# Moving the sample group of a GLA mixer from the front of its stage to between its last two groups, and loading two constants earlier

## The chip, the cores and the metric

The kernel runs on one core of a Trainium2 chip. The metric is the device time of one launch in microseconds (us), lower is better. Three runs of the kernel before took 3023.51, 3023.68 and 3024.13 us; the median is 3023.68.

The engines are named as in the profile: PE is TensorE's matrix multiplication, PEld its weight load, DVE VectorE, ACT ScalarE, POOL GpSimd, and SP SyncE, which in this kernel issues most of the DMAs. Each engine works through its own instructions in order and waits on semaphores for the others.

## What is computed

One layer of a hybrid decoder trunk, for a prompt of 2048 tokens and a sample group of 8 sequences of 8 tokens (64 tokens). Three mixers read the same projected stream: a gated DeltaNet (A), an RG-LRU (B) and a gated linear attention, GLA (C). Their outputs, side by side, go through one output projection with a layer norm, and then through a gated feed-forward block with a causal convolution (ConvFFN). The part that the change touches is mixer C and the output projection. Cut from the reference (chunks of 64 tokens; a chunk of the sample group is one sequence of 8):

```python
def step(S, inp):                       # GLA, one chunk
    qi, ki, vi, fi = inp
    b = jnp.cumsum(fi, axis=-2)
    ...
    att = jnp.einsum('bhik,bhjk,bhijk->bhij', qi, ki, dec)
    o = jnp.einsum('bhik,bhkv->bhiv', qi * jnp.exp(b), S) + jnp.einsum('bhij,bhjv->bhiv', att, vi)
    S_new = jnp.exp(b_last[..., 0, :])[..., None] * S + jnp.einsum('bhjk,bhjv->bhkv', ki * jnp.exp(b_last - b), vi)
    return S_new, o
...
heads = jnp.concatenate([oa, ob, oc], axis=-1)
x = layer_norm(ALPHA * x + heads @ w_out, ln1_g, ln1_b)
f, fconv_new = conv_ffn(x, st_fconv, ffn_w_up, ffn_conv_w, ffn_conv_b, ffn_w_down)
x = layer_norm(ALPHA * x + f, ln2_g, ln2_b)
```

The prompt starts from a state of zero and carries it from chunk to chunk. Each of the 8 sample sequences has a state of its own, given as input (`s_gla`) and returned (`o_glas`).

## The kernel before

`program` runs five stages: `setup`, `phase1` (the input projections), `window_a` (DeltaNet and RG-LRU), `window_c` (mixer C, output projection and first layer norm) and `phase3` (ConvFFN). The stages follow each other in the program, but a scheduler lays out each engine's instructions by priority and dependences, so work of neighbouring stages mixes. Only `phase3` is under `manual_schedule`, where the written order counts within the stage. What a tile waits for is decided by the pools: a tile that is placed where an earlier tile of a closed pool lay waits for all readers of that one.

**Mixer C (`Gla`).** The tokens are cut into groups: `G[0]` to `G[7]` with 256 prompt tokens each, and `G[8]` with the 64 sample tokens. `load` fetches a group's gates, keys, queries (`b`, `k`, `q`) and values (`v`). `prep` builds, head by head (six heads), the scaled copies of keys and queries at three levels (tiles `K1`, `Q1` and so on, filled by ACT and POOL in two sets of slots), takes the scores on PE (tile `s`, L1373), and copies them into `RC`; it transposes values (`pv`, L1394, into `XC`) and keys (`pk`, L1399, into `KC`) with the identity `c_ident`. `RC`, `XC` and `KC` are rings of two for the prompt's groups; the sample has its own `RCs`, `XCs`, `KCs`. `chain` runs the prompt's four chunks of a group in sequence: state product `cs` (L1427), outputs `po` (L1430), norm (L1205 to L1210, with a product by `ones`, L1206).

**The sample (`sample`)** is a generator with two parts. The first loads the eight states into a `room` of four tiles, takes the outputs (L1451 and L1453) and their norm. The second makes the new states: masked values, 8 x 6 matmuls `ss` (L1466) into one bank of PSUM with the tag `cs`, an addition on DVE, and the stores to `o_glas`. In before the room is four spare tiles of `Project` (`spare`: `mx`, `mh`, `ml`, `xt`).

**The output projection (`Project`).** `weights` loads the 8 blocks of `w_out` (`wos`, 512 KB each, three buffers shared with `x`) and splits each in two: `woh` on ACT (L1495), `wol` on POOL and DVE (L1496). A call P(t0) handles 128 tokens: ACT's cast `mh` and POOL's rest `ml` of the mixed heads `mx`, 48 matmuls `pm` (L320) in two halves, then DVE's residual and layer norm. P(2048) is the sample's call, P(0) to P(1920) the prompt's. `transposed` turns the result with the identity (`pt`, L1549), copies it out through the only buffer `xt` (L1550, ACT), and stores it to `s_x1T` (L1552, SP) for phase 3. The calls run at a much lower priority than the mixer, so the scheduler fills PE's gaps with them.

**The order in `window_c`** is `G[8]`, `G[0]`, ..., `G[7]`: the sample is prepared and put out first, the weights are loaded behind it, and its state sums come in G0's turn. The constants `ident` and `ones` for this stage are loaded into a pool `c3` that is opened after `Project`'s pools.

**The start of phase 3.** Its first pool `fx0` takes space that the closed pools of the earlier stages leave. `load_x(0)` loads eight input blocks `fxl00` to `fxl07` from `s_x1T` (the first five issued by POOL, the others by SP, L1666), ACT casts each into `fxh` (L1667), and DVE or, for the blocks 1, 4 and 7, POOL leaves the rest in `fxl` (L1668). The first weights `wh_g`, `wl_g`, `wh_v`, `wl_v` are split by ACT (L1614) and POOL (L1615). With them begin the matmuls `pug` and `puv` (L320).

Of the kernel before, what the change touches and what calls it, by code (L numbers as in the profile page):

```python
# [8 lines left out]
F32 = mybir.dt.float32  # L9
# [294 lines left out]
def load_consts(E, pool, names):  # L304
    t = {}
    for n in names:
        o, w = _CST[n]
        t[n] = pool.tile([128, w], F32, name="c_" + n)
        E.nc.sync.dma_start(t[n], E.d["consts"][:, o:o + w])
    return t  # L310
# [397 lines left out]
def deltanet(E, ctx, pools, need, ahead):  # L708
# [341 lines left out]
    for gs in pairs:  # L1050
        for g in gs:
            prep(g)
        inverse(gs)
        ahead(gs[0].pair)
        for g in gs:
            blocks(g)
        last = gs[-1].smp
        for g in (gs[0], *gs[2:], gs[1]):
            tokens(g)
            weights(g)  # L1060
            if g.b == 7:
                with tc.high_priority(-100):
                    sample()
            if not g.smp:
                chain(g)
# [147 lines left out]
class Gla:  # L1213
# [4 lines left out]
    def __init__(self, E, ctx):  # L1218
        nc, tc = E.nc, E.tc
        self.E = E  # L1220
        E.aset(LNEXP)
        early = ctx.enter_context(tc.tile_pool(name="ce", bufs=1))
        self.early = ctx.enter_context(tc.tile_pool(name="cf", bufs=2))
        pool = ctx.enter_context(tc.tile_pool(name="c1", bufs=1))
        self.tr = ctx.enter_context(tc.tile_pool(name="c2", bufs=2))
        self.pg = {t: ctx.enter_context(tc.tile_pool(name="c" + t, bufs=1, space=PSUM)) for t in ("s", "tk", "g")}
        self.C = load_consts(E, early, ["m2", "m3", "m2s", "bj", "i32"])

        def ring(name, n, c, w):
            return [pool.tile([128, 6, c, w], F32, name=f"{name}{i}") for i in range(n)]  # L1230

        self.RC, self.XC, self.KC = ring("RC", 2, 4, 64), ring("XC", 2, 4, 64), ring("KC", 2, 4, 32)
        sg = [early.tile([128, 6, 1, 64], F32, name="RCs")], ring("XCs", 1, 1, 64), ring("KCs", 1, 1, 32)
        self.slots = [{n: early.tile([128, 256], F32, name=f"{n}_{i}") for n in ("K1", "Q1", "K2", "Q2", "K3", "Q3")}
                      for i in range(2)]
        self.sls = [{n: early.tile([128, 64], F32, name=f"{n}_s{i}") for n in ("K2", "Q2")} for i in range(2)]

        self.KN = [{l: early.tile([128, 512 >> t], F32, name=f"KN{l}_{t}") for l in (1, 2, 3)} for t in range(2)]

        self.DD = [{l: early.tile([128, n, 6], F32, name=f"D{l}_{i}") for l, n in ((1, 4), (2, 16), (3, 64))}  # L1240
                   for i in range(2)]
        self.ebs = pool.tile([32, 6, 8], F32, name="ebs")
        for r in sg:
            nc.vector.memset(r[0][0:64], 0.0)
        nc.vector.memset(sg[0][0][64:], 0.0)
        for d in self.sls + self.KN + self.slots:
            for w in d.values():
                nc.gpsimd.memset(w, 0.0)
        for d in self.DD:
            for w in d.values():  # L1250
                nc.gpsimd.memset(w, 1.0)
        for w in self.RC + self.XC + self.KC:
            nc.gpsimd.memset(w[0:64], 0.0)
        self.G = []
        for g in range(9):
            o = Env()
            o.g, o.smp, o.t0 = g, g == 8, g * 256
            o.RC, o.XC, o.KC = (r[0] for r in sg) if o.smp else (r[g % 2] for r in (self.RC, self.XC, self.KC))
            o.nch = 1 if o.smp else 4
            o.n = 64 * o.nch  # L1260
            self.G.append(o)
# [158 lines left out]
    def chain(self, g):  # L1420
        nc = self.E.nc
        for c in range(4):
            if c % 2 == 0:
                po, z = self.outputs(g.t0 + 64 * c)
            ps = self.psum(f"cs{g.g}{c}", (32, 6, 64), "cs", 1)
            for h in range(6):
                nc.tensor.matmul(ps[:, h], g.KC[:, h, c], g.XC[:, h, c], start=True, stop=True)  # L1427
            for h in range(6):
                p, h2 = divmod(h, 2)
                nc.tensor.matmul(po[h2 * 64:(h2 + 1) * 64, p, c % 2 * 64:c % 2 * 64 + 64], g.XC[:, h, c],  # L1430
                                 g.RC[:, h, c], start=True, stop=True)
            if c < 3:
                nx = g.XC[0:32, :, c + 1]
            else:
                nx = self.G[g.g + 1 if g.g < 7 else 0].XC[0:32, :, 0]
            nc.scalar.copy(nx, ps)
            if g.g == 7 and c == 3:
                nc.sync.dma_start(self.E.d["o_glap"], nx)
            if c % 2 == 1:
                self.norm(po, z, g.t0 + 64 * (c - 1))  # L1440

    def sample(self, g, room):
        nc, E, C = self.E.nc, self.E, self.C
        S0 = big = room
        for i in range(4):
            nc.sync.dma_start(S0[i][0:32], E.d["s_gla"][:, 2 * i:2 * i + 2])
        po, z = self.outputs(g.t0)
        for h in range(6):
            p, h2 = divmod(h, 2)
            o = po[h2 * 64:(h2 + 1) * 64, p]  # L1450
            nc.tensor.matmul(o, g.XC[64:, h, 0], g.RC[64:, h, 0], start=True, stop=False)  # L1451
            for b in range(8):
                nc.tensor.matmul(o[:, b * 8:(b + 1) * 8], S0[b // 2][0:32, b % 2, h],  # L1453
                                 g.RC[0:32, h, 0, b * 8:(b + 1) * 8], start=False, stop=b == 7)
        self.norm(po, z, g.t0)
        yield
        for i in range(4):
            nc.vector.tensor_tensor(big[i][64:], g.XC[64:, None, :, 0].to_broadcast([64, 2, 6, 64]),
                                    C["bj"][64:, 2 * i:2 * i + 2, None, None].to_broadcast([64, 2, 6, 64]), op=OP.mult)
            nc.vector.tensor_tensor(S0[i][0:32], S0[i][0:32],  # L1460
                                    self.ebs[:, :, 2 * i:2 * i + 2, None].rearrange("p h b o -> p b h o")
                                    .to_broadcast([32, 2, 6, 64]), op=OP.mult)
            for b in range(2):
                ps = self.psum(f"ss{i}{b}", (32, 6, 64), "cs", 1)
                for h in range(6):
                    nc.tensor.matmul(ps[:, h], g.KC[64:, h, 0], big[i][64:, b, h], start=True, stop=True)  # L1466
                nc.vector.tensor_tensor(S0[i][0:32, b], S0[i][0:32, b], ps, op=OP.add)
            nc.sync.dma_start(E.d["o_glas"][:, 2 * i:2 * i + 2], S0[i][0:32])
        yield
# [6 lines left out]
class Project:  # L1476
# [13 lines left out]
    def weights(self):  # L1490
        E, nc = self.E, self.E.nc
        for k in range(KD):
# [2 lines left out]
            nc.scalar.copy(self.wh[:, k], st)  # L1495
            (nc.gpsimd if k % 2 else nc.vector).tensor_tensor(  # L1496
                self.wl[:, k], st, self.wh[:, k].bitcast(F32), op=OP.subtract)

    def spare(self):

        tags = [("mx", 2), ("mh", 2), ("ml", 2), ("xt", 1)]
        return [self.tr.tile([128, 2, 6, 64], F32, tag=t, bufs=b, name="sp" + t) for t, b in tags]

    def dest(self, t0):

# [49 lines left out]
def window_c(E):  # L1555

    with ExitStack() as ctx:
        C = Gla(E, ctx)
        P = Project(E, ctx)
        C.C.update(load_consts(E, ctx.enter_context(E.tc.tile_pool(name="c3", bufs=1)), ["ident", "ones"]))  # L1560
        room = P.spare()
        C.dest = P.dest
        order = [C.G[8]] + C.G[:8]
        C.load(order[0])
        for i, g in enumerate(order):
            if i < 8:
                C.load(order[i + 1])
            C.prep(g)
            if g.smp:
                smp = C.sample(g, room)  # L1570
                next(smp)
                P.weights()
            else:
                if g.g == 0:
                    next(smp)
                C.chain(g)
            for t0 in range(g.t0, g.t0 + g.n, 128):
                with E.tc.high_priority(-10 ** 5):
                    P(t0)
                    P.transposed(C.C["ident"], 1)  # L1580
        P.transposed(C.C["ident"])
# [373 lines left out]
def program(tc, dram):  # L1955

    E = Env()
    E.nc, E.tc, E.d = tc.nc, tc, dram
    with ExitStack() as ctx:
        setup(E, ctx)  # L1960
        phase1(E)
        window_a(E)
        window_c(E)
        phase3(E)
# [16 lines left out]
```

## Time and profile before

| what | number |
|---|---|
| median of three runs | 3023.68 us |
| profiled run, its own time | 3025.96 us |
| span of its profile, first to last instruction | 3024.2 us |
| mean granted clock of TensorE | 0.958 |
| PE busy | 2886.8 us (95%) |
| DVE, ACT, POOL busy | 1510.9 (50%), 1231.4 (41%), 844.2 us (28%) |
| first matmuls of P(2048) | 1083.41 us |
| first matmul of P(0) | 1133.94 us |
| first transposes behind the last projection matmul | 1493.23 us |

A row of the timeline gives the start, the duration, engine, line, operation, result and operands, shape and count of merged instructions, and in brackets how long the engine was idle before and what ended that. A name loses its number in the profile, so `pm` stands for all calls of P, and `c_ident` for the identity in each stage. The granted clock (PEclk) is the share of TensorE's full speed that the profile shows as granted. A window from 1040 to 1494 us covers mixer C and the projection; phase 3 takes the rest of the span, half of it all.

### The profile page before, as it was taken

Reading aid. Unit: us, or ns where it says so; the run is one execution under the profiler, and the core shown is the slowest. Engines: PE = TensorE matmul, PEld = TensorE weight load, DVE = VectorE, ACT = ScalarE, POOL = GpSimd, SP = SyncE. Lnnn points to the kernel's source line nnn. Section 1 sums busy time; section 2 is a strip of 40 time slices with the busy share of each in tenths; the row PEclk is TensorE's granted clock in tenths of the full one; section 3 lists DMA queues with packets and bytes.
Section 4 is the critical chain, followed back from the end, with each engine's and each line's share of the span. In section 5 each row is a group of like instructions: output and inputs, shape, how many; then the busy total and the mean of one; then the engine's idle time right before and its main releaser. Section 6 shows DMA issues by size and latency. Waiting matters only on the chain.

```text
span 3024.2 us, 45238 instructions
## 1 busy us (share of the span) xinstructions
PE 2886.8 (95%) x17755; PEld 2490.4 (82%) x17755; DVE 1510.9 (50%) x2454; ACT 1231.4 (41%) x2591; POOL 844.2 (28%) x898
## 2 busy tenths in 40 slices
PE   8999999788889799999899999999999999999998
PEld 7888789777779577767678888888889999999997
DVE  4564443577663676756533333333376443344436
ACT  4474443446653687766332222222232222222223
POOL 0000001734423545444222222222232222222224
PEclk9999999789999579999899999999999999999999
DMA  6221113533433443533531111111134111111111
GB/s 198 83 74 68 58 59 96 144 101 111 114 95 99 108 130 110 150 112 117 180 116 45 46 56 49 51 48 42 49 112 146 42 52 47 48 42 42 49 43 62
DMA packets 196508, 256.77 MB, mean 85 GB/s; under 512 B 43170, under 2 KB 162040, under 8 KB 196232
## 3 DMA queue, kind: packets, MB, share of 16 engines
q1 hardware_dynamic: 194168, 246.58, 26.6%
q0 software_dynamic: 1984, 7.12, 0.6%
q8 instruction: 140, 2.29, 0.3%
q14 instruction: 72, 0.59, 0.1%
q10 hardware_dynamic: 144, 0.20, 0.0%
HBM read 183.94 MB, written 60.08 MB: 81 GB/s over the span
## 4 chain that ended last, share of the span: by engine, by line
PE 60%; DVE 4%; ACT 2%; DMA 1%; issue 1%; POOL 1%; SPq 0%; DVEq 0%; POOLq 0%; ACTq 0%
PE pug L320 16%; PE pd L320 15%; PE puv L320 15%; PE pm L320 6%; PE s L1373 2%; DVE y L1788 1%; PE pd L1870 1%; PE cs L1427 1%; ACT Q L1360 1%; PE zp L1121 1%; PE po L1206 0%; PE zp L1122 0%; PE po L1430 0%; PE zp L1123 0%; DVE act L1724 0%
## 5 line engine op out<-in xcount | busy, mean ns | idle before, releaser
L1724 DVE SCALAR_TENSOR_TENSOR act<-G,cols,act 128x1024 f32<-128x1024 f32 (+1 forms) x132 | 123.6, 950 | 492.0 <-ACT act L1722 489.6
L1877 DVE TENSOR_TENSOR y<-y,pd 128x512 f32<-128x512 f32 x322 | 220.9, 687 | 203.2 <-PE pd L320 196.7
L1615 POOL TENSOR_TENSOR wl_d<-ws_d,wh_d 128x1024 fp32r<-128x1024 f32 x44 | 106.2, 2414 | 569.9 <-ACT wh_d L1614 523.1
L320 PE MATMUL pd<-wh_d,hh 128*128 128x512 f32 x704 | 215.4, 391 | 5.6 <-DVE y L1877 3.7
L320 PE MATMUL pd<-wh_d,hl 128*128 128x512 f32 x704 | 214.9, 390 | 0.0
L320 PE MATMUL pd<-wl_d,hh 128*128 128x512 f32 x704 | 214.6, 390 | 0.0
L1704 ACT COPY G<-pug 128x512 f32<-128x512 f32 (+2 forms) x110 | 55.0, 501 | 388.2 <-PE pug L320 388.2
L320 PE MATMUL pug<-fxh,wh_g 128*128 128x512 f32 (+2 forms) x880 | 198.0, 354 | 3.3 <-ACT wh_g L1614 2.6
L320 PE MATMUL puv<-fxh,wh_v 128*128 128x512 f32 (+2 forms) x880 | 196.4, 352 | 0.8 <-ACT wh_v L1614 0.8
L320 PE MATMUL puv<-fxh,wl_v 128*128 128x512 f32 (+2 forms) x880 | 196.2, 352 | 0.2 <-POOL wl_v L1615 0.2
L320 PE MATMUL puv<-fxl,wh_v 128*128 128x512 f32 (+2 forms) x880 | 196.0, 351 | 0.0
L320 PE MATMUL pug<-fxl,wh_g 128*128 128x512 f32 (+2 forms) x880 | 196.0, 351 | 0.0
L320 PE MATMUL pug<-fxh,wl_g 128*128 128x512 f32 (+2 forms) x880 | 195.9, 351 | 0.0
L320 PE MATMUL pm<-xh,wh 128*128 128x448 f32 (+1 forms) x800 | 181.9, 360 | 7.1 <-ACT xh L370 6.3
L1614 ACT CAST wh_d<-ws_d 128x1024 fp32r<-128x1024 f32 x44 | 45.8, 1040 | 337.5 <-PE pd L1870 173.3
L320 PE MATMUL pm<-xh,wl 128*128 128x448 f32 (+1 forms) x800 | 181.6, 359 | 0.0
L320 PE MATMUL pm<-xl,wh 128*128 128x448 f32 (+1 forms) x800 | 179.8, 358 | 0.5 <-DVE xl L371 0.4
L1766 DVE TENSOR_TENSOR hl<-act,hh 128x512 fp32r<-128x512 f32 (+2 forms) x110 | 124.0, 1128 | 99.5 <-ACT hh L1758 99.5
L320 PEld LDWEIGHTS pug<-fxh,wh_g 128*128 128x128 f32 x880 | 157.0, 189 | 19.0 <-ACT wh_g L1614 3.0
L320 PEld LDWEIGHTS puv<-fxh,wh_v 128*128 128x128 f32 x880 | 156.0, 188 | 14.9 <-ACT wh_v L1614 1.2
L320 PEld LDWEIGHTS pm<-xh,wh 128*128 128x128 f32 x800 | 144.4, 188 | 28.5 <-issue 10.1
L320 PEld LDWEIGHTS puv<-fxh,wl_v 128*128 128x128 f32 x880 | 155.6, 188 | 14.3 <-POOL wl_v L1615 0.6
(731 smaller groups left out, 6273.9 us busy)
## 6 DMA issues: line engine op xcount, KB each, us to landing
ws_d<-in_w_dn SPq DMA_DIRECT2D x44, 512.0 KB
ws_g<-in_w_up SPq DMA_DIRECT2D x43, 512.0 KB
ws_v<-in_w_up SPq DMA_DIRECT2D x43, 512.0 KB
zx<-in_xT SPq DMA_DIRECT2D x56, 256.0 KB
ws<-in_w_in SPq DMA_DIRECT2D x19, 512.0 KB
K<-KN SPq DMA_DIRECT2D x288, 32.0 KB
x<-in_x SPq DMA_DIRECT2D x16, 512.0 KB
s_x<-x SPq DMA_DIRECT2D x16, 512.0 KB
```

The source lines that it names most:

```text
L320: nc.tensor.matmul(ps, w[k], x[k], start=first and i == 0, stop=last and i == 3 * n - 1)
L1121: nc.tensor.matmul(ps, wh[:, k], xl, start=k == 0, stop=False)
L1360: nc.scalar.copy(v4(Q3[32 * a:32 * a + 32], 1)[:, :, a], v4(qq, 1)[:, :, a])
L1373: nc.tensor.matmul(ps[64:, c], K[:, i], Q[:, i], start=True, stop=True)
L1427: nc.tensor.matmul(ps[:, h], g.KC[:, h, c], g.XC[:, h, c], start=True, stop=True)
L1614: nc.scalar.copy(h, t)
L1615: nc.gpsimd.tensor_tensor(lo, t, h.bitcast(F32), op=OP.subtract)
L1704: nc.scalar.copy(G[:, 2 + o:2 + o + m], p[:, :m])
L1724: nc.vector.scalar_tensor_tensor(dst(act), src(i), taps[i], dst(act), op0=OP.mult, op1=OP.add)
L1766: nc.vector.tensor_tensor(dst, act[:, c], hh[:, c].bitcast(F32), op=OP.subtract)
L1788: nc.vector.scalar_tensor_tensor(y[:m, js], y[:m, js], mv[:m, tt, i:i + 1], a[:m, js], op0=op, op1=OP.add if i else OP.mult)
L1877: nc.vector.tensor_tensor(y, y, ps, op=OP.add)
```

## The change

In `window_c` the groups now run in the order `G[0]` to `G[6]`, `G[8]`, `G[7]`. The sample's first part comes in the turn of `G[8]`, its state sums after the chain of `G[7]`. The weights of the projection are loaded behind the preparation of the first group, which is now `G[0]`. The room for the sample's states is no longer spare tiles of `Project` but the halves of `RC[0]` and `XC[0]`, which are G6's. The state sums use the PSUM bank with the tag `tk`, that of the value and key transposes, instead of `cs`. The last state of the chain, which went to the buffer of `G[0]`, now goes to that of `G[7]` itself. The constants `ident` and `ones` are loaded with mixer C's other constants into its first pool `ce`.

```diff
--- before.py
+++ after.py
@@ -1224,7 +1224,7 @@
         pool = ctx.enter_context(tc.tile_pool(name="c1", bufs=1))
         self.tr = ctx.enter_context(tc.tile_pool(name="c2", bufs=2))
         self.pg = {t: ctx.enter_context(tc.tile_pool(name="c" + t, bufs=1, space=PSUM)) for t in ("s", "tk", "g")}
-        self.C = load_consts(E, early, ["m2", "m3", "m2s", "bj", "i32"])
+        self.C = load_consts(E, early, ["m2", "m3", "m2s", "bj", "i32", "ident", "ones"])
 
         def ring(name, n, c, w):
             return [pool.tile([128, 6, c, w], F32, name=f"{name}{i}") for i in range(n)]
@@ -1432,7 +1432,7 @@
             if c < 3:
                 nx = g.XC[0:32, :, c + 1]
             else:
-                nx = self.G[g.g + 1 if g.g < 7 else 0].XC[0:32, :, 0]
+                nx = self.G[min(g.g + 1, 7)].XC[0:32, :, 0]
             nc.scalar.copy(nx, ps)
             if g.g == 7 and c == 3:
                 nc.sync.dma_start(self.E.d["o_glap"], nx)
@@ -1461,7 +1461,7 @@
                                     self.ebs[:, :, 2 * i:2 * i + 2, None].rearrange("p h b o -> p b h o")
                                     .to_broadcast([32, 2, 6, 64]), op=OP.mult)
             for b in range(2):
-                ps = self.psum(f"ss{i}{b}", (32, 6, 64), "cs", 1)
+                ps = self.psum(f"ss{i}{b}", (32, 6, 64), "tk", 1)
                 for h in range(6):
                     nc.tensor.matmul(ps[:, h], g.KC[64:, h, 0], big[i][64:, b, h], start=True, stop=True)
                 nc.vector.tensor_tensor(S0[i][0:32, b], S0[i][0:32, b], ps, op=OP.add)
@@ -1495,11 +1495,6 @@
             nc.scalar.copy(self.wh[:, k], st)
             (nc.gpsimd if k % 2 else nc.vector).tensor_tensor(
                 self.wl[:, k], st, self.wh[:, k].bitcast(F32), op=OP.subtract)
-
-    def spare(self):
-
-        tags = [("mx", 2), ("mh", 2), ("ml", 2), ("xt", 1)]
-        return [self.tr.tile([128, 2, 6, 64], F32, tag=t, bufs=b, name="sp" + t) for t, b in tags]
 
     def dest(self, t0):
 
@@ -1557,23 +1552,25 @@
     with ExitStack() as ctx:
         C = Gla(E, ctx)
         P = Project(E, ctx)
-        C.C.update(load_consts(E, ctx.enter_context(E.tc.tile_pool(name="c3", bufs=1)), ["ident", "ones"]))
-        room = P.spare()
         C.dest = P.dest
-        order = [C.G[8]] + C.G[:8]
+
+        order = [*C.G[:7], C.G[8], C.G[7]]
+        room = [t.rearrange("p h c i -> p (h c i)")[:, i * 768:(i + 1) * 768].rearrange("p (b h i) -> p b h i", b=2, h=6)
+                for t in (C.RC[0], C.XC[0]) for i in range(2)]
         C.load(order[0])
         for i, g in enumerate(order):
-            if i < 8:
+            if i + 1 < len(order):
                 C.load(order[i + 1])
             C.prep(g)
+            if i == 0:
+                P.weights()
             if g.smp:
                 smp = C.sample(g, room)
                 next(smp)
-                P.weights()
             else:
-                if g.g == 0:
-                    next(smp)
                 C.chain(g)
+            if g.g == 7:
+                next(smp)
             for t0 in range(g.t0, g.t0 + g.n, 128):
                 with E.tc.high_priority(-10 ** 5):
                     P(t0)
```

How this moves the instructions is seen in the order of each engine. (The lines behind the change have numbers that are 3 to 5 lower.) First PE around the start of P(0), whose first matmuls are `pm00` and `pm01`; `s1_2` is the score of head 2 of group 1, `po256` the output of tokens 256 to 383. In before:

```order
L1373 MATMUL s2_0_11620<-Q1_0_9705,K1_0_9704 64x64 x4
L1430 MATMUL po256_11219<-RC1_9696,XC1_9698 64x64 x7
L1373 MATMUL s32_0_11621<-Q3_0_9709,K3_0_9708 64x64 x4
L1427 MATMUL cs13_11282<-XC1_9698,KC1_9700 32x64 x6
L1399 MATMUL pk21_11593<-c_ident_9792,kd1_2_11529 64x64 x4
L320 MATMUL pm00_10707<-woh_9780,mh0_10703 128x512 x8
```

and in the changed kernel:

```order
L1373 MATMUL s1_1_10620<-Q2_1_9717,K2_1_9716 64x64 x4
L1373 MATMUL s1_2_10658<-Q1_0_9709,K1_0_9708 64x64 x4
L1373 MATMUL s31_2_10659<-Q3_0_9713,K3_0_9712 64x64 x4
L1430 MATMUL po256_10789<-RC1_9700,XC1_9702 64x64
L1399 MATMUL pk21_11163<-c_ident_9695,kd1_2_11099 64x64 x4
L1427 MATMUL cs20_11400<-XC0_9701,KC0_9703 32x64 x4
L320 MATMUL pm00_10291<-woh_9784,mh0_10287 128x512 x6
```

P(0) stood behind scores of G2's head 0; now it stands behind those of G1's head 2. The sample's matmuls, which stood ahead of both in before, are not ahead of it now. They stand among G7's heads, with the state sums (`ss`) and P(2048) (`pm2048`) between the scores of `s7` and the outputs of the last 256 tokens (`po1792`, `po1920`):

```order
L320 MATMUL pm20481_14378<-woh_9784,ml2048_14349 128x512 x2
L1373 MATMUL s37_4_14716<-Q3_0_9713,K3_0_9712 64x64 x4
L1430 MATMUL po1792_14770<-RC1_9700,XC1_9702 64x64
L1430 MATMUL po1920_14816<-RC1_9700,XC1_9702 64x64
L1466 MATMUL ss30_14922<-XC0_9701,KCs0_9707 32x64 x6
L320 MATMUL pm20481_14378<-woh_9784,ml2048_14349 128x512 x2
L1373 MATMUL s7_4_14715<-Q2_0_9711,K2_0_9710 64x64 x4
L320 MATMUL pm20481_14378<-woh_9784,ml2048_14349 128x512 x4
L320 MATMUL pm20481_14378<-wol_9785,mh2048_14348 128x512 x8
```

Next PE where the projection ends and phase 3 begins (`pm19201` is the last half of P(1920), `pug` the first product of phase 3). In before:

```order
L320 MATMUL pm19201_15056<-wol_9781,mh1920_15026 128x512 x8
L1549 MATMUL pt17920_15093<-c_ident_9792,x1792_14886 128x128 x4
L1549 MATMUL pt17921_15099<-c_ident_9792,x1792_14886 128x128 x4
L320 MATMUL pug0_0_0_15226<-fxl00_15171,wh_g0_0_15164 128x512
L320 MATMUL pug0_0_0_15226<-fxh01_15175,wh_g0_0_15164 128x512
L320 MATMUL pug0_0_0_15226<-fxh01_15175,wl_g0_0_15165 128x512
```

and in the changed kernel:

```order
L320 MATMUL pm19201_15049<-wol_9785,mh1920_15019 128x512 x8
L1544 MATMUL pt17920_15086<-c_ident_9695,x1792_14803 128x128 x4
L1544 MATMUL pt17921_15092<-c_ident_9695,x1792_14803 128x128 x4
L1544 MATMUL pt19200_15100<-c_ident_9695,x1920_14850 128x128 x4
L1544 MATMUL pt19201_15106<-c_ident_9695,x1920_14850 128x128 x4
L320 MATMUL pug0_0_0_15218<-fxh00_15162,wh_g0_0_15156 128x512
L320 MATMUL pug0_0_0_15218<-fxh00_15162,wl_g0_0_15157 128x512
L320 MATMUL pug0_0_0_15218<-fxl00_15163,wh_g0_0_15156 128x512
```

In before two `pug` already stand further up, and 28 more come ahead of the last transposes `pt1920`. Now all four last transposes come first, and every `pug` is behind them. Last ACT at the same place; in before the casts `fxh` are spread among the copies, the last copies `xt1920` stand behind them all:

```order
L1550 COPY xt1792_15092<-pt17920_15093 128x512
L1550 COPY xt1792_15092<-pt17921_15099 128x512
L1667 CAST fxh05_15195<-fxl05_15196 128x1024
L1667 CAST fxh06_15200<-fxl06_15201 128x1024
L1667 CAST fxh07_15205<-fxl07_15206 128x1024
L1614 CAST wh_v0_0_15210<-ws_v0_0_15157 128x1024
L1179 ACTIVATE mv1920_15082<-mv1920_15082 128x1
L1180 ACTIVATE mv1920_15082<-mv1920_15082 128x1
L1550 COPY xt1920_15106<-pt19200_15107 128x512
L1550 COPY xt1920_15106<-pt19201_15113 128x512
```

and in the changed kernel:

```order
L1545 COPY xt1792_15085<-pt17920_15086 128x512
L1545 COPY xt1792_15085<-pt17921_15092 128x512
L1179 ACTIVATE mv1920_15075<-mv1920_15075 128x1
L1180 ACTIVATE mv1920_15075<-mv1920_15075 128x1
L1545 COPY xt1920_15099<-pt19200_15100 128x512
L1545 COPY xt1920_15099<-pt19201_15106 128x512
L1664 CAST fxh00_15162<-fxl00_15163 128x1024
L1664 CAST fxh01_15167<-fxl01_15168 128x1024
L1664 CAST fxh02_15172<-fxl02_15173 128x1024
```

All eight casts now stand behind the copies `xt1920`, each of which needs the buffer that the store of `xt1792` releases. On POOL the rows at this place are the same in both, with the loads `fxl00` and `fxl01` behind `ml1920`; but the first of them, which in before waited for early DMAs of mixer C alone, now also waits for PE's `pt19201`, the last reader of the identity.

## The prediction

> **What bounds the kernel now.** I read first the windows by stage (columns: busy us and instructions of each engine, then the granted clock, DMA share, GB/s), because the change touches only the stage of mixer C, from 1040 to 1494 us, and the hand-over to phase 3 behind it.
>
> ```profile
> core 0: us, PE busy (x) PEld busy (x) DVE busy (x) ACT busy (x) POOL busy (x), PEclk, DMA share, GB/s
> 1040.00:1090.00 50.00, 43.68 (x300) 35.34 (x299) 35.45 (x62) 31.78 (x85) 19.43 (x25) 0.51 0.62 184
> 1090.00:1134.00 44.00, 38.45 (x416) 30.28 (x414) 30.46 (x70) 34.38 (x102) 21.87 (x45) 0.96 0.33 92
> 1134.00:1300.00 166.00, 160.15 (x1225) 125.27 (x1225) 119.03 (x234) 119.57 (x352) 77.39 (x129) 0.99 0.45 130
> 1455.00:1494.00 39.00, 31.74 (x142) 23.58 (x142) 19.54 (x23) 13.39 (x24) 15.64 (x12) 0.82 0.53 175
> 1494.00:1530.00 36.00, 29.54 (x117) 23.18 (x118) 15.87 (x15) 14.48 (x21) 10.20 (x5) 0.91 0.51 156
> ```
>
> TensorE is the bound everywhere: 160.15 of 166 us in the middle. But from 1040 to 1090 it is busy at a granted clock of 0.51, so what stands there costs twice, and that is where the sample group stands. So I ask three things: what leaves the slow stretch, what it costs in the new place, and what becomes of the hand-over. Next the waits of PE from 1040 to 1134:
>
> ```profile
> PE pv L1394 <- DMA c_ident<-in_consts: 5.1, 1, 5.1
> PE s L1373 <- POOL Q L1351: 3.5, 2, 2.8
> ```
>
> The first wait is for the identity, loaded behind window A's last store; with the constant loaded early it is gone. The 3.5 us for POOL's `Q` belong to the prompt's heads and stay.
>
> **Part 1: what leaves the front.** The rows (line view and timeline of PE, same stretch):
>
> ```profile
> L1451 PE MATMUL po<-RCs,XCs x12: 310/338/366, 1046.8 to 1059.0; 64*64 64x64 f32 x12
> ```
>
> ```profile
> 1080.14 1.49 PE L1466 MATMUL ss<-spmh,KCs 64*32 64x64 f32 x12
> ...
> 1083.41 5.49 PE L320 MATMUL pm<-woh,mh 128*128 128x512 f32 x12 [0.53 <-ACT mh L1524]
> ...
> 1104.08 0.85 PE L1466 MATMUL ss<-spxt,KCs 64*32 64x64 f32 x12 [0.19 <-DVE spxt L1467]
> ...
> 1133.94 0.50 PE L320 MATMUL pm<-woh,mh 128*128 128x512 f32 x1
> ```
>
> ```profile
> L1373 PE MATMUL s<-Q,K 128*64 128x64 f32 x222 | 21.9, 259 | 4.1 <-POOL Q L1351 3.5 <-DVE RC L1379 0.5
> L1394 PE MATMUL pv<-c_ident,v 128*64 128x128 f32 x39 | 8.2, 333 | 5.8 <-DMA c_ident<-in_consts 5.1 <-ACT XCs L1395 0.3 <-ACT XC L1395 0.3
> ```
>
> - The sample's outputs: two L1451 matmuls a head; from the first head's pair to the sixth's (1046.8 to 1059.0) 12.2 us over 5.5 heads, 2.2 us a head, 13.2 us for six.
> - Its state sums: 96 matmuls, half of them at 1.49 us for 12 and half at 0.85: 4 x 1.49 + 4 x 0.85 = 9.4 us.
> - Its projection P(2048), 48 matmuls: the first 12 took 5.49 us at the slow clock; the other 36 came at full clock, 8 in about 1.8 us (the spacing of the rows in part 3), 8.2 us. Together 13.7.
> - Its scores (12 matmuls at 0.259), value and key transposes (6 at about 0.33) and two norm products (0.6 each): 6.3 us.
> - The wait for the identity: 5.1.
>
> That is 47.7 us of PE's time in front of the prompt's first projection P(0), which starts at 1133.94. The order in the changed kernel also lets P(0) begin some 8 us of prompt work sooner (behind head s1_2 instead of s2_0), which is only a swap and comes back later. So P(0) should start at about 1133.94 - 47.7 - 8 = 1078. Only the 47.7 are a gain. Bounds: if ACT, which between 1040 and 1090 is 31.78 of 50 us busy, gets the prompt's fills and the eight weight casts on top and holds P(0) to 1090, the gain is 12 less; if PE also drops the 3.5 us for POOL and gets its fast clock some 10 us sooner, it is 8 or 9 more.
>
> **Part 2: what it costs in its new place.** Between G6 and G7 the clock is 0.99 in the nearest long stretch, so the same work takes: P(2048) 48 x 1.8/8 = 10.9 us; outputs half of 13.2, 6.6; state sums 8 x 0.85 = 6.8; the rest 6.3 x 0.6 = 3.8. Sum 28.1 us. To this come waits which the trace doesn't show: the state sums now take turns with the value and key transposes in one bank of PSUM, and each must wait for its DVE addition; the sums' space (buffers of G6) must be free. From below nothing (G7's heads and P's matmuls fill PE between them, as the row 1134 to 1300 has 97% busy); from above eight turns of a DVE addition and a handshake, 10 us. I take 4, nearer to the row. The move alone thus gains 47.7 - 28.1 - 4 = about 16 us (12 less to 12 more by the two bounds): the last projection matmul comes at about 1477 instead of 1493.
>
> **Part 3: the hand-over.** Here the diff shows nothing and the order shows all. Call T the end of the last projection matmul, 1493.2 in before. PE there:
>
> ```profile
> 1491.41 1.98 PE L320 MATMUL pm<-wol,mh 128*128 128x512 f32 x8
> 1493.23 0.60 PE L1549 MATMUL pt<-c_ident,x 128*128 128x128 f32 x4
> ...
> 1502.69 0.51 PE L320 MATMUL puv<-fxh,wh_v 128*128 128x512 f32 x1 [0.80 <-ACT wh_v L1614]
> 1505.57 1.94 PE L1549 MATMUL pt<-c_ident,x 128*128 128x128 f32 x8 [2.38 <-DVE x L1186]
> 1507.68 0.80 PE L320 MATMUL puv<-fxh,wl_v 128*128 128x512 f32 x1 [0.18 <-POOL wl_v L1615]
> ```
>
> Before, PE has phase 3's work from T + 2 on, and from T + 14.45 it runs without a stop, with 30 `pug` and one `puv` matmul done. That rests on `fxl00` to `fxl04`, phase 3's first input rows, being loaded and split while mixer C still runs. In the changed kernel the identity lies in an earlier pool, and its space is what phase 3's first pool takes over: the load of `fxl00` on POOL now waits for the last transpose on PE that reads it (`pt19201`), and all that stands behind it on POOL, ACT and PE waits with it. On ACT the casts `fxh00` to `fxh07` moved behind the copies `xt1920`. The rows for the durations:
>
> ```profile
> 1476.59 1.64 POOL L1666 DMA_DIRECT2D fxl<-s_x1T  x3
> 1485.01 2.38 POOL L1668 TENSOR_TENSOR fxl<-fxl,fxh 128x1024 fp32r<-128x1024 f32 x1 [6.78 <-ACT fxh L1667]
> 1501.77 2.57 POOL L1668 TENSOR_TENSOR fxl<-fxl,fxh 128x1024 fp32r<-128x1024 f32 x1 [14.38 <-ACT fxh L1667]
> 1504.30 3.33 POOL L1615 TENSOR_TENSOR wl_v<-ws_v,wh_v 128x1024 fp32r<-128x1024 f32 x1
> ```
>
> ```profile
> 1501.59 1.04 ACT L1614 CAST wh_v<-ws_v 128x1024 fp32r<-128x1024 f32 x1
> ...
> 1509.37 1.07 ACT L1550 COPY xt<-pt 128x512 f32<-128x512 f32 x2 [6.40 <-DMA s_x1T<-xt]
> ```
>
> ```profile
> 1502.62 0.38 SPq L1552 DMA_DIRECT2D s_x1T<-xt  x1
> ```
>
> ```profile
> fxl<-s_x1T POOLq DMA_DIRECT2D x5, 512.0 KB, 4.7
> ```
>
> Step by step, from T: the last transposes end at T + 7 (the layer norm of 1920 no longer stands behind DVE's `fxl` subtractions). The copies `xt1920` need the one `xt` buffer, which the store of `xt1792` holds: in before it was issued at T + 9.4 and released ACT at T + 16.1, and nothing ahead of it on SP changes. So the copies end at T + 17.2, `fxh00` and `fxh01` at T + 19.2 (1.0 each), POOL's subtraction of `fxl01` at T + 21.6 (2.4). Only then does POOL issue `fxl02` to `fxl04` (0.55 each), which land 4.7 us after issue, from T + 26.9. Six casts, ACT being in order: to T + 33; `wh_v` T + 34. POOL subtracts `fxl04` and `fxl07`, to T + 35.4, and `wl_v`, to T + 38 (2.6). PE then has the same 31 matmuls behind it and runs on. So the hand-over takes 38 - 14.45 = 23.5 us more. Bounds: if the store of `xt1792` lands by T + 9.6, all is 6.5 earlier, 17 more; if both rounds of loads take 8 instead of 4.7 us, with the 512 KB loads of weights beside them, 30 more. I add 0.5 for slow matmuls after the hole: 24.
>
> A sentence on the page: "TensorE: Matmul & The Clock Gate" of the Trainium skill (Part 1: The HAM clock gate) says that the throttled clock is the default and is left after a window of about 3.4 us of sustained activity. By that rule the first P matmuls of phase 3 would cost an estimated 1.7 us more, and G0's dense heads in the changed front could run at full clock from the start; the trace agrees with the time that the 12 matmuls at 1083.41 needed, but not with the stretch before them, busy 87% at 0.51. Another, "DMA: Bandwidth & Descriptors" (Anatomy of one DMA), gives about 2.0 us and bytes over 436 GB/s for a transfer issued by POOL, an estimated 3.2 us for 512 KB; with it in place of the row's 4.7 the hand-over would be 1.5 us shorter. The row decides.
>
> **Sum.** -47.7 + 28.1 + 4 + 24 = +8.4 us. The profiled run took 3025.96 us by its own time (span 3024.2); that makes it 3034.4 there, and 3032 against the median of 3023.68.
>
> **Rivals.**
> - ACT late: the casts of the output weights and the prompt's fills hold P(0) to 1090. For it: ACT is 34.38 of 44 us busy from 1090 to 1134, where PE still waits for fills. Against it: it has little to do from 1040 to 1090. Net 8 + 12 = 20, time 3044, and with the upper bound of the hand-over 3051.
> - It nets out: the store of `xt1792` goes sooner, since fewer `fxl` loads crowd the queues before T, and the hand-over costs 17. For it: in before that store waits 9 us behind loads on SP. Against it: those loads stay ahead of it. Net +1, 3025.
> - Faster, on the other side: the clock. If PE's granted clock is 1.00 by 1060 instead of 1090, because G0's heads and the transposes run without the 5.1 us hole and P(0) comes early, then of some 36 us to 1078, 87% busy, half is saved, up to 15 us. It decides the sign from about 1062 on. Net 8 - 15 = -7, with the lower hand-over -14: 3010 to 3017. Against it: 87% busy at 0.51 before, with the same kind of small matmuls.
>
> **How the numbers follow.** A measurement of this kernel tells 0.2% (6 us) from nothing. Chances: the forecast, +6 to +16, 0.42; ACT late or the upper hand-over, 0.16; netting out, within 6, 0.24; the clock, faster by over 6, 0.18. So faster 0.18, same 0.24, slower 0.58. The range takes the bounds of the front (12 either way) with the hand-over (17 to 30) less the rarest corners: -13 to +28, 3011 to 3051. The forecast's own range is 3030 to 3040.
>
> **What would show it.** Right: no wait for `c_ident` at the front; P(0) near 1078; the sample's matmuls about 28 us among G6's and G7's at full clock; the last projection at about 1477; then a hole in PE of some 10 us before the first `pug`, and `puv` without stop from T + 38; POOL's first `fxl` load released by PE's `pt`. Wrong: the first `fxl` load before T; a start of P(0) after 1090; the state sums waiting over 10 us in their bank; a clock of 1.00 well before P(0).

## The result, and the profile after

The changed kernel took 3048.03 us, the median of four runs (3044.98 to 3052.0), beside 3023.9 for the kernel before in the same job; the ratio is 1.0078 with a 95% interval of 1.0061 to 1.0096. It is 24 us slower. The forecast was slower, by 8; 3048 lies inside the range of 3011 to 3051, but outside the forecast's own 3030 to 3040.

The profiled run has a span of 3049.2 us, 25.0 more than before. First the same windows by stage (columns as before):

```profile
core 0: us, PE busy (x) PEld busy (x) DVE busy (x) ACT busy (x) POOL busy (x), PEclk, DMA share, GB/s
1040.00:1090.00 50.00, 37.84 (x350) 29.42 (x350) 31.98 (x62) 42.29 (x108) 33.88 (x45) 0.86 0.64 189
1090.00:1134.00 44.00, 36.77 (x298) 27.57 (x296) 30.56 (x62) 29.97 (x90) 23.81 (x42) 0.92 0.42 127
1134.00:1300.00 166.00, 152.20 (x1201) 118.99 (x1200) 111.16 (x243) 124.60 (x372) 83.73 (x144) 0.95 0.40 119
1455.00:1494.00 39.00, 32.47 (x176) 25.00 (x174) 18.15 (x26) 10.55 (x22) 8.31 (x5) 0.87 0.33 100
1494.00:1530.00 36.00, 13.57 (x39) 8.08 (x39) 12.35 (x8) 10.86 (x15) 12.14 (x9) 0.62 0.63 208
```

Two rows differ most. From 1494 to 1530 PE is busy 13.57 of 36 us instead of 29.54: that is the hand-over. And from 1040 to 1090 the clock is 0.86 instead of 0.51, but PE is busy 37.84 instead of 43.68, and ACT 42.29 instead of 31.78. What PE waits for there (same view as before, 1040 to 1134):

```profile
PE cs L1427 <- ACT XC L1436: 4.3, 3, 2.9
PE s L1373 <- ACT RC L1376: 3.0, 2, 2.2
PE s L1373 <- DMA K<-KN: 1.9, 1, 1.9
PE po L1206 <- ACT z L1205: 1.7, 2, 1.5
```

The wait for the identity is gone; in its place stand many small ones for ACT, for the keys' DMAs and for others. P(0) starts here (PE's timeline):

```profile
1077.83 3.02 PE L320 MATMUL pm<-woh,mh 128*128 128x512 f32 x12
```

That is 56 us sooner than before. Yet at the end nothing is left of it. PE at the hand-over:

```profile
1490.54 1.98 PE L320 MATMUL pm<-wol,mh 128*128 128x512 f32 x8
1492.36 0.60 PE L1544 MATMUL pt<-c_ident,x 128*128 128x128 f32 x4
...
1496.99 1.59 PE L1544 MATMUL pt<-c_ident,x 128*128 128x128 f32 x8 [3.04 <-DVE x L1186]
1511.56 0.79 PE L320 MATMUL pug<-fxh,wh_g 128*128 128x512 f32 x1 [12.98 <-ACT fxh L1664]
...
1531.64 0.80 PE L320 MATMUL puv<-fxh,wl_v 128*128 128x512 f32 x1 [2.46 <-POOL wl_v L1612]
```

From here on T is the end of the last projection row, and the hand-over the time from T to the `puv` from which PE runs on. Before: T 1493.4 and 14.3 us. After: T 1492.5 and 39.1 us. So of the 25.0 us by which the profiled span grew, 24.8 came from the hand-over; all that changed ahead of T gained 0.9, and 1.1 was lost behind the hand-over. The four runs of the changed kernel lie in two pairs, near 3045 and near 3051.5, and the profiled one is of the longer pair; what makes the two is open. A gain of 0.9 can't be told from nothing.

What PE did from the start of the program to T, before and then changed:

```profile
0.00:1493.39 1493.39, 1377.11 (x10263) 1157.08 (x10264) 865.08 (x1596) 838.44 (x1974) 457.87 (x676) 0.92 0.37 108
0.00:1492.52 1492.52, 1367.57 (x10261) 1149.96 (x10262) 855.21 (x1596) 835.20 (x1969) 459.86 (x669) 0.93 0.36 107
```

PE's busy time to T fell by 9.5 us, and its idle time (T less the busy time) rose by 8.7, from 116.3 to 125.0. By the windows it rose by 15.5 between 1040 and 1300 and fell by 6.8 elsewhere.

ACT and POOL of the changed kernel at the hand-over:

```profile
1509.49 1.07 ACT L1545 COPY xt<-pt 128x512 f32<-128x512 f32 x2 [14.57 <-DMA s_x1T<-xt]
1510.45 2.00 ACT L1664 CAST fxh<-fxl 128x1024 fp32r<-128x1024 f32 x2
1518.93 1.04 ACT L1664 CAST fxh<-fxl 128x1024 fp32r<-128x1024 f32 x1 [6.48 <-DMA fxl<-s_x1T]
...
1525.26 1.05 ACT L1611 CAST wh_v<-ws_v 128x1024 fp32r<-128x1024 f32 x1
```

```profile
1498.88 1.11 POOL L1663 DMA_DIRECT2D fxl<-s_x1T  x2 [20.02 <-DMA fxl<-s_x1T]
1512.54 2.50 POOL L1665 TENSOR_TENSOR fxl<-fxl,fxh 128x1024 fp32r<-128x1024 f32 x1 [12.54 <-ACT fxh L1664]
1514.99 1.65 POOL L1663 DMA_DIRECT2D fxl<-s_x1T  x3
...
1528.27 3.32 POOL L1612 TENSOR_TENSOR wl_v<-ws_v,wh_v 128x1024 fp32r<-128x1024 f32 x1
```

POOL sat idle for 20 us and issued the first two loads at 1498.88, 0.3 us after PE's last transpose (1496.99 + 1.59 = 1498.58). The profile names a DMA as the releaser; the program's own wait is on that transpose, and the times agree with it. In `old_order_early_pool`, below, the same load comes 0.3 us behind the last transpose too, and there the profile names PE.

### The profile page after: what moved, and what is told of

The parts are those of the page before. It is cut to its first block, busy times and chain, and to the rows that moved or that the text cites. A ratio compares the mean times of both kernels' runs of the same rounds, so it can differ in the third digit from the quotient of the medians.

```text
span 3049.2 us, 45248 instructions
## 1 busy us (share of the span) xinstructions
PE 2884.0 (95%) x17755; PEld 2486.0 (82%) x17755; DVE 1503.9 (49%) x2454; ACT 1232.9 (40%) x2591; POOL 854.2 (28%) x898
## 5 line engine op out<-in xcount | busy, mean ns | idle before, releaser
L320 PEld LDWEIGHTS pug<-fxl,wh_g 128*128 128x128 f32 x880 | 155.8, 188 | 18.3 <-POOL fxl L1665 2.8
L320 PEld LDWEIGHTS pug<-fxh,wl_g 128*128 128x128 f32 x880 | 156.8, 189 | 14.5 <-POOL wl_g L1612 0.4
```

Source lines behind the costliest of these rows:

```text
L320: nc.tensor.matmul(ps, w[k], x[k], start=first and i == 0, stop=last and i == 3 * n - 1)
```

## The experiments

Each was timed beside the kernel before on the same chip (its median there was 3023.7 to 3024.7). These kernels spread over 3 to 13 us from run to run, and T and the hand-over are each read from one profile. Together they account for each run's difference in time from the kernel that it was made from, within about 4 us. Differences of T of 3 us or less decide nothing, and one of 4 or 5 is weak evidence.

| run | time, us | ratio (95%) | T | hand-over |
|---|---|---|---|---|
| kernel before | 3023.9 | | 1493.4 | 14.3 |
| changed kernel | 3048.0 | 1.0061 to 1.0096 | 1492.5 | 39.1 |
| old_order_early_pool | 3052.9 | 1.0090 to 1.0121 | 1497.1 | 40.0 |
| new_order_late_const | 3030.3 | 1.0012 to 1.0030 | 1497.2 | 17.5 |
| new_order_own_pool | 3034.0 | 1.0023 to 1.0050 | 1490.1 | 26.1 |
| old_order_own_pool | 3042.3 | 1.0053 to 1.0083 | 1501.5 | 23.9 |
| new_order_cs_bank | 3050.9 | 1.0078 to 1.0109 | 1490.2 | 41.4 |
| before_no_sample | 3009.1 | 0.9935 to 0.9967 | 1475.6 | 17.3 |
| after_no_sample | 3028.2 | 1.0001 to 1.0021 | 1469.8 | 40.1 |
| before_outputs_twice | 3042.6 | 1.0039 to 1.0080 | 1509.9 | 14.4 |
| after_outputs_twice | 3067.5 | 1.0118 to 1.0159 | 1506.9 | 40.2 |
| new_order_woh_on_dve | 3040.3 | 1.0042 to 1.0076 | 1496.6 | 26.0 |
| own_pool_rest_on_dve | 3035.2 | 1.0022 to 1.0048 | 1494.6 | 25.8 |
| sample_second | 3035.6 | 1.0021 to 1.0052 | 1492.4 | 24.6 |

**The place of the constants (hand-over).** Two edits, one on each kernel.

```diff
 old_order_early_pool, against before
-        self.C = load_consts(E, early, ["m2", "m3", "m2s", "bj", "i32"])
+        self.C = load_consts(E, early, ["m2", "m3", "m2s", "bj", "i32", "ident", "ones"])
-        C.C.update(load_consts(E, ctx.enter_context(E.tc.tile_pool(name="c3", bufs=1)), ["ident", "ones"]))
 new_order_late_const, against the changed kernel
-        self.C = load_consts(E, early, ["m2", "m3", "m2s", "bj", "i32", "ident", "ones"])
+        self.C = load_consts(E, early, ["m2", "m3", "m2s", "bj", "i32"])
...
+        C.C.update(load_consts(E, ctx.enter_context(E.tc.tile_pool(name="c3", bufs=1)), ["ident", "ones"]))
         C.dest = P.dest
```

> The kernel before with one part of the change alone: identity and ones loaded with the other constants into the first pool, the old order of the groups. Theory A: the hand-over takes 39 us instead of 14.5, the wait of 5.1 us for the identity goes, time 3043 to 3049. Theory B: the hand-over stays at 14.5 us, time 3019 to 3024.

> The changed kernel's order of groups, room and bank, but identity and ones loaded as in the kernel before (late, into the pool behind the projection's). The order alone. Theory A: the hand-over is back at about 14.5 us. If the early identity is not what gives the front its gain, the last projection matmul comes within 3 us of the changed kernel's 1492.5 and the time is 3020 to 3027; if the front needs it, it comes at 1497 or later and the time is 3028 or more.

The early constants alone, with the old order, make the whole hand-over late (40.0 us, time 3052.9); the new order alone leaves it at 17.5. PE of the first of the two:

```profile
1516.77 0.79 PE L320 MATMUL pug<-fxh,wh_g 128*128 128x512 f32 x1 [13.89 <-ACT fxh L1666]
...
1537.08 0.50 PE L320 MATMUL puv<-fxh,wl_v 128*128 128x512 f32 x1 [2.48 <-POOL wl_v L1614]
```

And its last transposes, with POOL's first load behind them:

```profile
1501.54 1.34 PE L1549 MATMUL pt<-c_ident,x 128*128 128x128 f32 x8 [3.04 <-DVE x L1186]
```

```profile
1503.18 1.11 POOL L1665 DMA_DIRECT2D fxl<-s_x1T  x2 [23.11 <-PE pt L1549]
```

It is the same hole as in the changed kernel. Theory A holds, theory B falls, although 3052.9 lies above its 3043 to 3049. The new order with late constants falls into the second of its branches (T at 1497.2, 3030.3): T came 5 later than in the changed kernel, so the front there does seem to use the early identity.

The four kernels make a square. With late constants the new order moves T from 1493.4 to 1497.2 and costs 6 us of time; with early constants in the first pool it moves T from 1497.1 to 1492.5. So by these profiles neither half of the change brings T forward alone, and the move of the sample gains something only where the identity is early. The small pool below says the same (1501.5 to 1490.1).

**The constants early, but elsewhere.**

```diff
+        cid = ctx.enter_context(tc.tile_pool(name="ci", bufs=1))
...
+        self.C.update(load_consts(E, cid, ["ident", "ones"]))
```

The pool `ci` is opened right behind `c2`; the load into the old place is dropped.

> The changed kernel, but the identity and the ones lie in a small pool of their own behind the transposes' pool, loaded just as early. Theory A (the hand-over is late because of the place of the identity, whose space phase 3's first block load takes): PE runs without a stop from about 15 us behind the last projection matmul again instead of 39.3, time about 3024 (3019 to 3029). Theory B (the hand-over is late because the sample's projection and sums come just ahead of it): it stays at 35 us or more, time 3043 to 3050.

> The kernel before, identity and ones loaded early, but in the small pool of their own. It prices the wait of 5.1 us for the identity alone. If PE's time is what bounds the front (as the prediction had it): 5 us less, about 3019. If the head's chain over ACT and POOL bounds it, which goes on beside the sample's matmuls: within 2 us of 3024. Under theory A the hand-over is at 15 us in either case.

The hand-over fell to 26.1 and 23.9 us, not to 15, and both times (3034.0, 3042.3) lie above what was expected. The place moves the hand-over, but `ci` seems to lie where phase 3's block 5 comes: SP's load of `fxl05` now comes right behind the last transpose instead of the last projection matmul. The wait of 5.1 us for the identity brought nothing in the old order: without it T came 8 us later, not 5 sooner. That is not the price of the wait alone, since the scheduler also laid PE's instructions otherwise: 89 score matmuls stand ahead of the sample's outputs there, 105 in before.

**What holds the rest of that hand-over.**

```diff
-                (nc.gpsimd if k % 3 == 1 else nc.vector).tensor_tensor(
+                (nc.gpsimd if k in (1, 4) else nc.vector).tensor_tensor(
```

> The changed kernel with the constants in their own pool (3034.0, hand-over 26 us), and the rest of phase 3's input block 7 left to DVE instead of POOL. If the remaining 12 us of that hand-over come from POOL's split of the first value weights standing behind block 7, which SP can load only once the last transpose has read the identity, the hand-over falls to 15 to 18 us and the time to 3024 to 3027. If something else holds it, it stays above 22 us and the time above 3030.

Nothing changed (25.8), so my reason was wrong. The rows of ACT, POOL and SP show why:

```profile
1515.81 1.04 ACT L1666 CAST fxh<-fxl 128x1024 fp32r<-128x1024 f32 x1 [1.77 <-DMA fxl<-s_x1T]
1516.76 1.04 ACT L1613 CAST wh_v<-ws_v 128x1024 fp32r<-128x1024 f32 x1
```

```profile
1517.87 2.44 POOL L1614 TENSOR_TENSOR wl_v<-ws_v,wh_v 128x1024 fp32r<-128x1024 f32 x1 [20.81 <-ACT wh_v L1613]
```

```profile
1507.34 0.80 SPq L1665 DMA_DIRECT2D fxl<-s_x1T  x2
```

POOL is free for 20.81 us and waits for `wh_v`; ACT has that cast behind the casts of blocks 5 to 7, and SP issues those loads only at 1507.34, when the last transpose is done (1507.3). So ACT's order passes the wait on, not POOL's. Whether `wh_v` ahead of those casts would repair it was not tried.

**The bank of the state sums.**

```diff
-                ps = self.psum(f"ss{i}{b}", (32, 6, 64), "tk", 1)
+                ps = self.psum(f"ss{i}{b}", (32, 6, 64), "cs", 1)
```

> The changed kernel with the state sums back in the bank of the chain's state products. If the turns in the transposes' bank cost what the prediction charged or more, the last projection matmul comes 3 to 10 us sooner and the time is 3038 to 3045; if they cost next to nothing, within 3 us of the changed kernel, 3045 to 3051.

The time is 3050.9, the interval overlaps that of the changed kernel, and T came 2.3 sooner, within what T can tell: the bank costs nothing that shows.

**What the sample costs in either place.** `before_no_sample` and `after_no_sample` run `G[0]` to `G[7]` alone and leave the sample's results out. The edit of the second, with the parts that hang on it left out here:

```diff
-        order = [*C.G[:7], C.G[8], C.G[7]]
+        order = C.G[:8]
...
+    E.nc.sync.dma_start(E.s["x1"][T:TT], E.d["x"][T:TT])
+    E.nc.sync.dma_start(E.s["x1T1"][:, 1024:1088], E.d["xT"][:, T:TT])
```

> The kernel before without mixer C's sample group: its outputs, its state sums and its projection are left out (the sample's rows of x are copied on in their place). It prices the sample at the front. If the sample cost there what PE spent on it and the wait (the prediction's 47.7 us), the last projection matmul comes at about 1446 and the time is about 2976; if the prompt's heads, filled by ACT and POOL one after the other, went on beside it, the price is about 33 us: 1460 and 2990.

> The changed kernel without the sample group, with its early constants in the first pool. It prices the sample in its new place: 33 us (the prediction had 32), the last projection matmul at about 1459.5, the hand-over still at 39 us, time about 3015. If the sums' bank or the space of G6 made it dearer, it comes earlier than 1455.

Both expectations were too high. Without the sample at the front T came 1493.4 - 1475.6 = 17.8 us sooner, neither 47.7 nor 33; without it in the late place 1492.5 - 1469.8 = 22.7. PE from the start to T, first without the front sample, then without the late one:

```profile
0.00:1475.57 1475.57, 1347.76 (x9972) 1139.95 (x9973) 843.38 (x1537) 821.47 (x1893) 457.74 (x654) 0.92 0.36 108
0.00:1469.78 1469.78, 1348.21 (x9970) 1137.46 (x9971) 838.54 (x1537) 816.05 (x1888) 448.72 (x648) 0.92 0.36 107
```

At the front PE's busy time fell by 29.4 us, not by the 42.6 of work that the prediction counted, and its idle time rose by 11.5. In the late place the busy time fell by 19.4 and the idle time by 3.4.

These are not prices of the sample alone. The scheduler laid out the stage before anew as well: the last of the state products of `window_a` on PE (L1026) starts at 1040.4 instead of 1021.8 us in the first, and at 1041.3 instead of 1031.5 in the second. The window of `before_no_sample` that belongs beside the first rows of before:

```profile
1040.00:1090.00 50.00, 34.84 (x297) 26.26 (x297) 28.48 (x59) 40.11 (x102) 23.02 (x43) 0.66 0.68 200
```

PE, which was busy 43.68 of these 50 us, is now busy 34.84 and waits for the rest, while ACT goes from 31.78 to 40.11.

**More of the same work.** The other way round, the sample's outputs computed twice:

```diff
-        for h in range(6):
+        for h in (*range(6), *range(6)):
```

> The kernel before with the sample's outputs computed twice (the second pass writes the same numbers): 96 + 12 matmuls more, 13.2 us of PE's time at the front. If PE's time bounds the front, as the prediction had it, the last projection matmul comes 13 us later, time 3037. If the front waits for the heads' fills anyway, it comes at most 5 us later, time 3024 to 3029.

> The changed kernel with the sample's outputs computed twice: 6.6 us of PE's time at full clock in the late place. If PE bounds it there, 5 to 7 us later (3050 to 3056); if it fills waits there too, within 3 us of the changed kernel's 3045 to 3052.

At the front T moved by 16.5 us for an estimated 13.2 of work: PE's busy time to T rose by 11.7 and its idle time by 4.8. So added work counts in full there. In the late place T moved by 14.4, twice the 6.6 that were estimated at full clock: the busy time rose by 16.1 and the idle time fell by 1.7. Both times came out above what either branch expected. The windows of `after_outputs_twice` where that work runs:

```profile
1400.00:1410.00 10.00, 10.00 (x76) 7.97 (x76) 3.46 (x10) 5.79 (x16) 2.71 (x3) 1.00 0.39 120
1410.00:1420.00 10.00, 10.00 (x93) 9.06 (x91) 0.00 (x0) 0.24 (x1) 0.61 (x2) 0.63 0.03 8
1420.00:1430.00 10.00, 10.00 (x63) 8.81 (x63) 5.37 (x8) 2.51 (x8) 1.74 (x3) 0.52 0.06 15
```

PE is busy without a gap, and the granted clock falls to 0.63 and 0.52. From 1410.52 to 1424.46 PE runs nothing but the sample's output matmuls. One head of them took 1.28 us at first (1410.52 to 1411.80) and 2.20 a little later (1413.46 to 1415.66): so the slow clock costs these 1.7 times, not twice as the prediction had it, and it came down while they ran.

**Which filler bounds the front.** The eight casts of `w_out` on DVE instead of ACT, on the kernel with the own pool:

```diff
-            nc.scalar.copy(self.wh[:, k], st)
+            nc.vector.tensor_copy(self.wh[:, k], st)
```

> The run with the constants in their own pool (3034.0; last projection matmul at 1490.1), with the eight casts of the projection's weights (1.04 us each) moved from ACT to DVE. If ACT's chain of fills sets the pace of the front, the heads come 4 to 8 us sooner and the time is 3026 to 3030; if not, it stays within 3031 to 3037.

It got slower (3040.3 against 3034.0; T 1496.6 against 1490.1), beyond either branch. But PE has a new wait from 1040 to 1134, for the casts themselves, which come late from DVE:

```profile
PE pm L320 <- DVE woh L1497: 5.3, 1, 5.3
```

So taking the casts from ACT this way doesn't help, but the run doesn't tell whether ACT paces the front. Which of the fills does stays open.

**The sample second.** On `own_pool_rest_on_dve`, the order `G[0]`, `G[8]`, `G[1]` to `G[7]`, the sums ahead of G1's chain:

```diff
-        order = [*C.G[:7], C.G[8], C.G[7]]
+        order = [C.G[0], C.G[8], *C.G[1:8]]
...
+                if g.g == 1:
+                    next(smp)
                 C.chain(g)
-            if g.g == 7:
-                next(smp)
```

> As the run before it (own pool, block 7 on DVE), but the sample group second, between G0 and G1, its sums ahead of G1's chain. If its PE work hides beside the heads' fills at the front, where it cost 18 us, as against 23 late, the last projection matmul comes at 1484 to 1489 and the time is 3016 to 3021. If it only takes PE from the heads, 1492 or later and 3024 or more.

T is 1492.4 and the time 3035.6, the same within the spread as with the sample late (1494.6 and 3035.2). With the sample first and the constants in the same small pool T was 1501.5 (`old_order_own_pool`). No version run here that computes everything beats the kernel before.

## Why the prediction was right in sign and short in size

- **Hand-over, +24: right, step by step.** Measured 39.1 - 14.3 = 24.8. The steps from T were: copies `xt1920` done at 17.2 (measured 18.1 by the row at 1509.49), `fxh00` and `fxh01` at 19.2 (20.0), POOL's subtraction at 21.6 (22.5), `fxh02` from 26.9 (26.4), `wh_v` at 34 (33.8), `wl_v` at 38 (39.1). That its cause is the place of the identity, and not the order of the groups, the first two runs showed. The sign of the forecast was right because of this term.
- **P(0) near 1078: right number, wrong use.** It started at 1077.83. The hit is in part luck: without the front sample P(0) starts at 1100.2, 34 us sooner than before and not 47.7. And `before_no_sample` ends the stage 18 us sooner than before, while the changed kernel, which starts P(0) 56 sooner, ends it 0.9 sooner. The start of a filler says nothing of the stage's end.
- **-47.7 at the front: the step that failed.** I summed what PE spends on the sample there, 42.6 us of work and the wait of 5.1 for the identity, and took both as gained in full. With the late place that made 42.6 - 28.1 = 14.5 us less busy time to T and 5.1 - 4 = 1.1 less idle time. Measured were 9.5 us less busy time and 8.7 more idle time. The wait for the identity went, but many small waits for ACT and others came in its place between 1040 and 1300. The omission runs point the same way: T fell by 17.8 us without the sample, and by 23.6 (1493.4 to 1469.8) without it and with early constants. The doubling showed that added work counts in full; the time of removed work did not come back in full. The chains of fills and copies that go on beside it are the likely reason; which of them takes over is not shown. "TensorE is the bound everywhere" was true of 160.15 of 166 us in the middle, but not of 38.45 of 44 or 31.74 of 39 in the rows beside it. PE's own waits for `Q`, whose heads are filled by ACT and POOL one after the other, stood in the quoted list and could have warned.
- **+28.1 + 4 in the late place: too dear.** By the omission it was 22.7, of which 19.4 were busy time; why the busy time was that much less than 28.1 is open. The full clock that I charged did not hold: in the changed kernel it was 0.58 from 1390 to 1400, where part of the sample's outputs run. The 4 us for the bank had no row behind them, and the run that undid the bank did not find them, within the 3 us that T can tell.
- Together: 47.7 - 23.6 = 24.1 too much gain, less 32.1 - 22.7 = 9.4 too much cost, makes 14.7, which is the distance between the forecast's -15.6 for T and the measured -0.9. The two terms pass over the same run, so they must add up to it; they sort the error and prove nothing.
- **The rival of the clock came true in the main and did not pay.** The clock was 0.86 from 1040 to 1090 instead of 0.51, though not steadily: 1.00 from 1060 to 1065, then 0.74 and 0.58 in the next two stretches of 5 us. PE turned the time into waits. The Trainium skill ("TensorE: Matmul & The Clock Gate", Part 1: The HAM clock gate) says that the throttled clock is the default and that sustained activity of about 3.4 us releases it. The trace agrees from 1060 to 1065, busy 4.90 of 5 us at 1.00, but not in the stretch of small matmuls in `after_outputs_twice`, busy 10.00 of 10 us at 0.63 and 0.52; the measurement decides.
- **The rival in which ACT is late** gave the right time by another way: P(0) was not held. Against it I had put that ACT has little to do from 1040 to 1090; it was busy 31.78 of those 50 us in before, and 42.29 in the changed kernel.

## What to carry to other kernels

Work taken off the busiest engine need not come back as time: other chains run beside it. Leave the work out in a trial, and compare busy and idle time of that engine before and after; but look first whether the scheduler laid out other stages anew. When a constant or any small tile is loaded earlier, look where its new place lies and who takes that space next: one late reader of 512 bytes a partition held up a whole stage's first loads. And an early start of a low-priority filler is no gain by itself.

## What was not expected of the hardware

PE busy without a gap did not keep the granted clock up here. A stretch of matmuls with operands of 64x64 and 32x8 elements fell to 0.63 and 0.52 within 20 us after 1.00 (the windows of `after_outputs_twice` above), and 6.6 us of such work, as estimated at full clock, moved the end of the stage by 14.4. In before the same holds where the sample's outputs stand: from 1050 to 1070 PE was busy 20.00 of 20 us at 0.50. What in these matmuls lets the clock fall is not shown.
